# Output projection with its whole weight on chip, one token tile after another, and block-sum transfers issued in other places

## The chip, the cores and the metric

The kernel runs on one core of a Trainium2 chip. The time is the device time of one execution, in microseconds (us); less is better. The engines are PE (TensorE, matmuls and transposes), DVE (VectorE), ACT (ScalarE), POOL (GpSimd) and SP (SyncE, which issues most of the transfers here). PEclk is the clock that PE was granted, as a share of 2.4 GHz.

## What is computed

One block of a streaming encoder over 1024 tokens of width 1024, in float32. Three mixers (a gated convolution, differential attention in four heads, gated linear attention, GLA) read one normed input; then comes the output projection, a second norm, and an MLP of 4096 hidden columns:

```python
def reference(x, ln1_g, w_in, ..., w_out, ln2_g, w_mlp1, w_mlp2):
    h = rms_norm(x, ln1_g[l])
    z = h @ w_in[l]
    ...
    y = jnp.concatenate([y_conv, y_diff, y_gla], axis=-1)
    x = x + y @ w_out[l]
    h2 = rms_norm(x, ln2_g[l])
    x = x + jnp.square(jax.nn.relu(h2 @ w_mlp1[l])) @ w_mlp2[l]
    return x
```

## The kernel before, in words

**Precision and matmuls.** A float32 operand is split into a high part (`hi`, cast by ACT, line 136) and a low part (`lo`, the rest, by DVE, line 137). A product is three matmuls (`mm3`, lines 155 to 158): high by low, high by high, low by high, all added into one PSUM bank. Weights come from DRAM to a staging tile of 512 KB (`stage()`, the tag "st", two buffers), are split from there into `hi` and `lo` tiles (four buffers of each tag) and the staging buffer is free for the next load. All of these loads are issued on SP's queue in one order.

**Stages.** Norm and transposes of x into hT; projections and GLA (lines 352 to 516, with the q and k projections woven in); four attention heads (line 529), whose results go to DRAM (`ydram`); the convolution; then the part that matters here. `yT`, the mixers' result transposed and split, is loaded from ydram for six of its eight 128-row blocks and computed for two (lines 668 to 680).

**Output projection (lines 724 to 734).** The loop runs over four column blocks `nb` of 256 columns; each takes one weight (two staged pieces of w_out, 512 rows by 256 columns, line 144) and inside it goes over the eight token tiles `tt`. A step is 24 matmuls of 256 columns, the addition to the residual `x1[tt]` on DVE, the sum of squares on ACT, and for nb < 3 one `next_sum`. The tile `g2` with the norm's gain takes a buffer of the tag "st". In the last column block, `h2_tile(tt)` follows each step: statistics, scaling by DVE (`xn`), eight transposes on PE, a copy into the blocks b11, b21, b12, b22, a store of x1 to DRAM (`x1d`), and for the first four tiles differences and splits for H6 and H5. `h2_sums` makes the other operands of the MLP: H3, H7, H2, H4, H1.

**MLP.** The first product runs block-wise with seven products per block q (i = 6, 5, 3, 7, 2, 4, 1) of 24 matmuls with 512 columns; each needs one staged weight piece (`w1_operand`, line 757). The products 6 and 5 of q = 0 and 1 come first (NPRE = 2), the first of them together with the last tiles' transposes. Then the second product (`pso`).

**Block sums.** Some of the MLP's operands are sums of blocks of w_mlp1 and w_mlp2, built in DRAM by transfers that POOL issues: copies and accumulating transfers of 1 MB, 64 steps in a fixed order (`BlockSums.steps`, lines 111 to 119). `next_sum(when)` (line 128) lets POOL copy one element of a tile, so that POOL waits for that tile, and then issues the next step. Before, 8 steps are paced by the GLA output tiles (every second of 16), 32 by the attention (eight per head) and 24 by the projection.

Of the kernel before, what the change touches and what calls it, by code (L numbers as in the profile page):

```python
# [9 lines left out]
F32 = mybir.dt.float32  # L10
F32R = mybir.dt.float32r
# [25 lines left out]
def hybrid_block(ctx, tc, x, ln1_g, w_in, conv_w, q_norm_g, k_norm_g, diff_lambda, diff_subln_g,  # L37
# [316 lines left out]
    for tt in range(NT):  # L354
        ps = gemm_b(wb, hT, tt)
        nc.scalar.copy(gv[:, tt, :], ps[:, 0:256])
    wb = load_w(w_in, C_GK, 256)
# [116 lines left out]
    def gla_out(g):  # L474
# [18 lines left out]
        if g % 2 == 1:  # L493
            next_sum(ssg[0:1, tt * 4 + hh:tt * 4 + hh + 1])
# [172 lines left out]
    wo0 = load_w(w_out, 0, 256)  # L667
# [20 lines left out]
    x1 = [xp.tile([P, D], F32, name=f"x1_{tt}") for tt in range(NT)]  # L688
# [5 lines left out]

    b21, b11, b12, b22 = act_f32("b21", "ah"), act_f32("b11", "ah"), act_f32("b12", "al"), act_f32("b22", "al")
    hb = ((b11, b21), (b12, b22))
    H = {i: act_pair(actp, f"H{i}") for i in (6, 5)}
    g2 = wpool.tile([P, D], F32, name="g2", tag="st", bufs=2)
    nc.sync.dma_start(g2, ln2_g[0:1, :].broadcast_to([P, D]))
    for tt in range(NT):  # L700
        nc.sync.dma_start(x1[tt], x2[tt * P:(tt + 1) * P, :])
    ss2 = xp.tile([P, NT, 4], F32, name="ss2")

    def h2_tile(tt):
        r = norm_stats(ss2[:, tt, :], 4, xp)
# [11 lines left out]
        if th == 0:  # L717
            d6 = xp.tile([P, 4, P], F32, name="d6", tag="xn", bufs=2)
            nc.vector.tensor_tensor(d6, b11[:, :, osl], b21[:, :, osl], op=ALU.subtract)
            split(*[v[:, :, osl] for v in H[6]], d6)  # L720
            split(*[v[:, :, osl] for v in H[5]], b21[:, :, osl])
        return t_.ins

    for nb in range(4):
        wb = wo0 if nb == 0 else load_w(w_out, nb * 256, 256)
        for tt in range(NT):
            ps = gemm_b(wb, yT, tt, 256, (6, 7, 2, 3, 4, 5, 0, 1))
            xv = x1[tt][:, nb * 256:(nb + 1) * 256]
            nc.vector.tensor_tensor(xv, xv, ps[:, 0:256], op=ALU.add)
            nc.scalar.activation(ps[:, 0:256], xv, AF.Square, accum_out=ss2[:, tt, nb:nb + 1])  # L730
            if nb < 3:
                next_sum(ss2[0:1, tt, nb:nb + 1])
            if nb == 3 and tt < NT - 1:
                h2_tile(tt)


    H.update({i: act_pair(yp, f"H{i}") for i in (3, 7, 4, 2)})

    def h2_sums():
        for i in range(4):  # L740
            o = slice(i * P, (i + 1) * P)
            v11, v12, v21, v22 = (b[:, :, o] for b in (b11, b12, b21, b22))
            split(*[v[:, :, o] for v in H[3]], v12)
            split(*[v[:, :, o] for v in H[7]], v22)
            nc.vector.tensor_tensor(v11, v11, v12, op=ALU.subtract)
            nc.vector.tensor_tensor(v21, v21, v11, op=ALU.subtract)
            nc.vector.tensor_tensor(v22, v22, v21, op=ALU.subtract)
            split(*[v[:, :, o] for v in H[2]], v22)
            split(*[v[:, :, o] for v in H[4]], v21)
        H[1] = act_pair(actp, "H1")  # L750
        for i in range(4):
            o = slice(i * P, (i + 1) * P)
            split(*[v[:, :, o] for v in H[1]], b11[:, :, o])
# [27 lines left out]
    pre = []  # L781
    w = w1_operand(0, 6)
    pre.append([prod(w, e, 6, "mm", 3) for e in range(2)])
    w = w1_operand(0, 5)
    with tc.issue_after(last_mm.ins):
        h2_end = h2_tile(NT - 1)
    with tc.issue_after(h2_end):
        pre.append([prod(w, e, 5, "s", 2) for e in range(2)])
# [39 lines left out]
    for q in range(NPRE):  # L828
        p6, p5 = pre if q == 0 else (prods(q, 6), prods(q, 5))
        first[q] = [out65(2 * q + e, p6[e], p5[e]) for e in range(2)]  # L830
# [149 lines left out]
```

## Time and profile before

| | before |
|---|---|
| median of 3 runs | 1267.23 us (1264.94 to 1267.30) |
| the profiled execution: time, span | 1265.83 us, 1264.1 us |
| PE busy, share of the span | 1197.6 us, 95% |
| DVE, ACT, POOL busy | 743.8, 522.8, 65.7 us |
| mean granted clock | 0.972 |
| chain that ended last, by engine | PE 78%, DMA 10%, DVE 6%, ACT 4% |
| of it, loads of w_out | 6% |

The span runs from the first to the last instruction; the profiled execution's own time is a little longer. A chain is followed back from the last instruction, at each step to what released it. Matmul records overlap on PE, so that a busy PE is not a PE at its peak.

### The profile page before, as it was taken

How to read it: one execution, taken by the hardware profiler on the slowest of the kernel's cores; microseconds unless marked ns; L12 is line 12 of the kernel's file. 1: busy time of each engine (PE TensorE's matmuls, PEld its weight loads, DVE VectorE, ACT ScalarE, POOL GpSimd, SP SyncE). 2: the span in 40 equal slices, each digit the busy share in tenths (PEclk: the TensorE clock that was granted, in tenths of full speed). 3: DMA queues.
4: the chain of work that ended last, by engine and by line, in shares of the span. 5: the costliest groups of instructions: out<-in, count | busy, mean ns of one | idle time of the engine just before them, and what ended most of it. 6: DMA issues, size and time to landing. Idle time of an engine off the chain costs nothing.

```text
span 1264.1 us, 17602 instructions
## 1 busy us (share of the span) xinstructions
PE 1197.6 (95%) x6803; PEld 1029.7 (81%) x6803; DVE 743.8 (59%) x1366; ACT 522.8 (41%) x1019; POOL 65.7 (5%) x147
## 2 busy tenths in 40 slices
PE   6999999999999999676689999999999999999998
PEld 6897899998988788576668888888888888888887
DVE  6616654568677873111597866776666555554553
ACT  6621233557566642111475343344433333333332
POOL 1000000020102112122000000000000000000000
PEclk8999999999999999778789999999999999999999
DMA  6211244197819778999734656565599995655000
GB/s 203 84 34 34 68 163 163 46 211 237 184 50 220 211 227 262 217 267 266 194 125 162 220 184 203 192 204 173 180 315 353 387 363 200 228 210 197 32 34 33
DMA packets 118961, 231.92 MB, mean 183 GB/s; under 512 B 7357, under 2 KB 53470, under 8 KB 115550
## 3 DMA queue, kind: packets, MB, share of 16 engines
q1 hardware_dynamic: 104286, 163.69, 38.1%
q0 software_dynamic: 14592, 67.11, 22.0%
q8 instruction: 53, 0.87, 0.3%
q14 instruction: 30, 0.25, 0.1%
HBM read 189.89 MB, written 108.00 MB: 236 GB/s over the span
## 4 chain that ended last, share of the span: by engine, by line
PE 78%; DMA 10%; DVE 6%; ACT 4%; issue 1%; SPq 1%; ACTq 0%; DVEq 0%
PE pso L158 8%; PE pso L156 8%; PE pso L157 8%; PE psp L156 8%; PE psp L157 8%; PE psp L158 8%; DMA wst<-in_w_out_dram 6%; PE ps_mm L156 6%; PE ps_mm L158 6%; PE ps_mm L157 6%; PE ps_av L605 3%; DMA wst<-in_w_mlp_dram 2%; PE ps_tr L597 1%; PE ps_s L575 1%; DMA wst<-ydram 1%; PE ps_s L576 1%
## 5 line engine op out<-in xcount | busy, mean ns | idle before, releaser
L157 PE MATMUL pso<-o2h 128*128 128x512 f32 x448 | 174.3, 389 | 0.0
L156 PE MATMUL pso<-o2l,o2h 128*128 128x512 f32 x448 | 174.3, 389 | 0.0
L158 PE MATMUL pso<-o2h,o2l 128*128 128x512 f32 x448 | 174.3, 389 | 0.0
L156 PE MATMUL ps_mm<-wlo,hTh 128*128 128x256 f32 (+1 forms) x512 | 147.8, 289 | 3.8 <-ACT hTh L201 3.8
L137 DVE TENSOR_TENSOR o2l<-f,o2h 128x1024 fp32r<-128x1024 f32 x56 | 68.6, 1225 | 139.4 <-ACT o2h L136 139.4
L157 PE MATMUL ps_mm<-whi,hTh 128*128 128x256 f32 (+1 forms) x512 | 147.1, 287 | 0.0
L158 PE MATMUL ps_mm<-whi,hTl 128*128 128x256 f32 (+1 forms) x512 | 146.2, 286 | 0.0
L136 ACT CAST o2h<-f 128x1024 fp32r<-128x1024 f32 x56 | 58.8, 1051 | 190.5 <-PE pso L157 186.6
L156 PE MATMUL ps_mm<-wlo,yTh 128*128 128x256 f32 x256 | 80.2, 313 | 32.5 <-ACT ps_mm L730 26.8
L137 DVE TENSOR_TENSOR wlo<-wst,whi 128x1024 fp32r<-128x1024 f32 x34 | 41.6, 1224 | 114.5 <-ACT whi L136 112.0
L136 ACT CAST w1h<-wst 128x1024 fp32r<-128x1024 f32 x56 | 58.9, 1053 | 106.8 <-PE psp L157 86.9
L156 PEld LDWEIGHTS ps_mm<-wlo,hTh 128*128 128x128 f32 x512 | 97.0, 190 | 7.0 <-ACT hTh L201 4.7
L157 PEld LDWEIGHTS pso<-o2h 128*128 128x128 f32 x448 | 84.1, 188 | 17.6
L158 PEld LDWEIGHTS pso<-o2h,o2l 128*128 128x128 f32 x448 | 84.1, 188 | 17.5
L156 PEld LDWEIGHTS pso<-o2l,o2h 128*128 128x128 f32 x448 | 84.1, 188 | 17.3
L158 PEld LDWEIGHTS ps_mm<-whi,hTl 128*128 128x128 f32 x512 | 97.4, 190 | 0.7 <-DVE hTl L202 0.2
L157 PEld LDWEIGHTS ps_mm<-whi,hTh 128*128 128x128 f32 x512 | 97.1, 190 | 0.9 <-issue 0.3
L815 DVE TENSOR_TENSOR s<-psp,s 128x512 f32<-128x512 f32 x96 | 64.7, 689 | 51.0 <-PE psp L158 46.0
L137 DVE TENSOR_TENSOR w1l<-wst,w1h 128x1024 fp32r<-128x1024 f32 x56 | 68.4, 1221 | 35.1 <-ACT w1h L136 35.1
L156 PEld LDWEIGHTS ps_mm<-wlo,yTh 128*128 128x128 f32 x256 | 55.5, 217 | 33.8 <-ACT ps_mm L730 27.9
L158 PE MATMUL ps_mm<-whi,yTl 128*128 128x256 f32 x256 | 78.3, 306 | 0.0
L157 PE MATMUL ps_mm<-whi,yTh 128*128 128x256 f32 x256 | 78.3, 306 | 0.0
(284 smaller groups left out, 2631.5 us busy)
## 6 DMA issues: line engine op xcount, KB each, us to landing
f<-fdram SPq DMA_DIRECT2D x28, 1024.0 KB
w1s<-in_w_mlp_dram POOLq DMA_DIRECT2D x24, 1024.0 KB, 9.8
w2s<-in_w_mlp_dram POOLq DMA_DIRECT2D x24, 1024.0 KB, 17.6
wst<-w1s SPq DMA_DIRECT2D x32, 512.0 KB
w<-w2s SPq DMA_DIRECT2D x16, 1024.0 KB
wst<-in_w_in_dram SPq DMA_DIRECT2D x26, 512.0 KB
wst<-in_w_mlp_dram SPq DMA_DIRECT2D x24, 512.0 KB
fdram<-s SPq DMA_DIRECT2D x48, 256.0 KB
```

The lines of the kernel that those rows point to most:

```text
L136: nc.scalar.copy(hi, src)
L137: return nc.vector.tensor_tensor(lo, src, hi.bitcast(F32), op=ALU.subtract)
L156: nc.tensor.matmul(ps, lh, rl, start=first, stop=False)
L157: nc.tensor.matmul(ps, lh, rh, start=False, stop=False)
L158: return nc.tensor.matmul(ps, ll, rh, start=False, stop=last)
L575: nc.tensor.matmul(ps[:, 0:w], qi, kll[c][:, j * 512:j * 512 + w], start=True, stop=False)
L576: nc.tensor.matmul(ps[:, 0:w], qi, khh[c][:, j * 512:j * 512 + w], start=False, stop=True)
L597: nc.tensor.transpose(tp[:, b * P:(b + 1) * P], pc[0][:, (b0 + b) * P:(b0 + b + 1) * P], ident)
L605: nc.tensor.matmul(av[:, 0:P], aT[:, b * P:(b + 1) * P], v[:, kb, hh * P:hh * P + P], start=(kb == 0), stop=(kb == i))
L815: nc.vector.tensor_tensor(dst, a_, b_, op=op)
```

## The change

The projection now goes over the token tiles, with two halves `nh` of 512 columns each. The weight is loaded in eight pieces of 256 rows by 512 columns (`load_wo`): the four of the first half into the tiles "hi" and "lo", the four of the second half into tiles that hT has left. The first three token tiles take the first half one after another, then the second half; from tile 3 on, each tile takes both. `h2_tile` of a finished tile comes under the matmuls of the next. x1 has four buffers instead of eight and each tile is loaded when it is needed; `g2` has a tile of its own. Splits for H6 and H5 are collected after tile 3, differences are made per tile from tile 4 on, and four weights of the MLP's first products are loaded ahead. Of the block sums, the 24 of the projection are gone: 8 are paced by the gv projection, 16 instead of 8 by the GLA tiles, 32 by the attention as before, and 8 by the MLP's blocks q.

```diff
@@ -354,6 +354,7 @@
     for tt in range(NT):
         ps = gemm_b(wb, hT, tt)
         nc.scalar.copy(gv[:, tt, :], ps[:, 0:256])
+        next_sum(gv[0:1, tt, 0:1])
@@ -490,8 +491,7 @@
-        if g % 2 == 1:
-            next_sum(ssg[0:1, tt * 4 + hh:tt * 4 + hh + 1])
+        next_sum(ssg[0:1, tt * 4 + hh:tt * 4 + hh + 1])
@@ -664,7 +664,19 @@
-    wo0 = load_w(w_out, 0, 256)
+    def load_wo(j, nh, hi, lo):
+        st = stage().rearrange("p (c n) -> p c n", c=2)
+        nc.sync.dma_start(st, w_out[j * 256:(j + 1) * 256, nh * 512:nh * 512 + 512].rearrange("(c p) n -> p c n", p=P))
+        split(hi, lo, st)
+        return hi, lo
+    def load_wo0(j):
+        return load_wo(j, 0, wpool.tile([P, 2, 512], F32R, name="woh", tag="hi", bufs=4),
+                       wpool.tile([P, 2, 512], F32R, name="wol", tag="lo", bufs=4))
+    wo = [{j: load_wo0(j) for j in (3, 1)}, {}]
     yT = act_tiles(yp, "yT")
     for kc in (6, 7, 2, 3, 4, 5):
         st = stage()[:, 0:T]
@@ -685,24 +697,35 @@
-    x1 = [xp.tile([P, D], F32, name=f"x1_{tt}") for tt in range(NT)]
...
+    wo[0].update({j: load_wo0(j) for j in (2, 0)})
+    x1 = {}
+    def x1_tile(tt):
+        x1[tt] = xp.tile([P, D], F32, name="x1", tag="x1", bufs=4)
+        nc.sync.dma_start(x1[tt], x2[tt * P:(tt + 1) * P, :])
+    for tt in range(2):
+        x1_tile(tt)
+    wo1 = [act_pair(actp, "wo1") for kh in range(2)]
+    for j in (3, 1, 2, 0):
+        js = slice((j % 2) * 2, (j % 2) * 2 + 2)
+        wo[1][j] = load_wo(j, 1, wo1[j // 2][0][:, js, :], wo1[j // 2][1][:, js, :])
+    x1_tile(2)
     b21, b11, b12, b22 = act_f32("b21", "ah"), act_f32("b11", "ah"), act_f32("b12", "al"), act_f32("b22", "al")
     hb = ((b11, b21), (b12, b22))
-    H = {i: act_pair(actp, f"H{i}") for i in (6, 5)}
-    g2 = wpool.tile([P, D], F32, name="g2", tag="st", bufs=2)
+    H = {}
+    g2 = xp.tile([P, D], F32, name="g2")
     nc.sync.dma_start(g2, ln2_g[0:1, :].broadcast_to([P, D]))
-    for tt in range(NT):
-        nc.sync.dma_start(x1[tt], x2[tt * P:(tt + 1) * P, :])
-    ss2 = xp.tile([P, NT, 4], F32, name="ss2")
+    ss2 = xp.tile([P, NT, 2], F32, name="ss2")
@@ -714,43 +737,70 @@
-        if th == 0:
-            d6 = xp.tile([P, 4, P], F32, name="d6", tag="xn", bufs=2)
...
-    for nb in range(4):
-        wb = wo0 if nb == 0 else load_w(w_out, nb * 256, 256)
-        for tt in range(NT):
-            ps = gemm_b(wb, yT, tt, 256, (6, 7, 2, 3, 4, 5, 0, 1))
...
-            nc.scalar.activation(ps[:, 0:256], xv, AF.Square, accum_out=ss2[:, tt, nb:nb + 1])
-            if nb < 3:
-                next_sum(ss2[0:1, tt, nb:nb + 1])
-            if nb == 3 and tt < NT - 1:
-                h2_tile(tt)
-    H.update({i: act_pair(yp, f"H{i}") for i in (3, 7, 4, 2)})
-    def h2_sums():
+    def h2_first():
+        for i in (6, 5):
+            H[i] = act_pair(yp, f"H{i}")
         for i in range(4):
             o = slice(i * P, (i + 1) * P)
-            v11, v12, v21, v22 = (b[:, :, o] for b in (b11, b12, b21, b22))
-            split(*[v[:, :, o] for v in H[3]], v12)
-            split(*[v[:, :, o] for v in H[7]], v22)
-            nc.vector.tensor_tensor(v11, v11, v12, op=ALU.subtract)
-            nc.vector.tensor_tensor(v21, v21, v11, op=ALU.subtract)
-            nc.vector.tensor_tensor(v22, v22, v21, op=ALU.subtract)
-            split(*[v[:, :, o] for v in H[2]], v22)
-            split(*[v[:, :, o] for v in H[4]], v21)
+            d6 = xp.tile([P, 4, P], F32, name="d6", tag="xn", bufs=2)
+            nc.vector.tensor_tensor(d6, b11[:, :, o], b21[:, :, o], op=ALU.subtract)
+            split(*[v[:, :, o] for v in H[6]], d6)
+            split(*[v[:, :, o] for v in H[5]], b21[:, :, o])
+    def h2_diffs(i):
+        o = slice(i * P, (i + 1) * P)
+        nc.vector.tensor_tensor(b11[:, :, o], b11[:, :, o], b12[:, :, o], op=ALU.subtract)
+        nc.vector.tensor_tensor(b21[:, :, o], b21[:, :, o], b11[:, :, o], op=ALU.subtract)
+    def gemm_o(tt, nh):
+        ps = ps_mm()
+        th, o = tt // 4, (tt % 4) * P
+        ks = (6, 7, 2, 3, 4, 5, 0, 1)
+        for kc in ks:
+            hi, lo = wo[nh][kc // 2]
+            ah, al = yT[th][kc // 4]
+            mm3(ps, ah[:, kc % 4, o:o + P], al[:, kc % 4, o:o + P], hi[:, kc % 2, :], lo[:, kc % 2, :],
+                kc == ks[0], kc == ks[-1])
+        return ps
+    NB = 3
+    waiting = []
+    for tt, nh in [(t, h) for h in range(2) for t in range(NB)] + [(t, h) for t in range(NB, NT) for h in range(2)]:
+        if tt not in x1:
+            x1_tile(tt)
+        ps = gemm_o(tt, nh)
+        xv = x1[tt][:, nh * 512:nh * 512 + 512]
+        nc.vector.tensor_tensor(xv, xv, ps, op=ALU.add)
+        nc.scalar.activation(ps, xv, AF.Square, accum_out=ss2[:, tt, nh:nh + 1])
+        if waiting:
+            t = waiting.pop(0)
+            h2_tile(t)
+            if t == 3:
+                h2_first()
+            if t >= 4:
+                h2_diffs(t - 4)
+        if nh == 1:
+            waiting.append(tt)
+    def h2_sums():
+        h2_diffs(3)
+        for i in (3, 7):
+            H[i] = act_pair(yp, f"H{i}")
+        H[4] = act_pair(actp, "H4")
+        H[2] = act_pair(actp, "H2")
+        parts = (slice(0, 3 * P), slice(3 * P, 4 * P))
+        for o in parts:
+            split(*[v[:, :, o] for v in H[3]], b12[:, :, o])
+        for o in parts:
+            split(*[v[:, :, o] for v in H[7]], b22[:, :, o])
+        nc.vector.tensor_tensor(b22, b22, b21, op=ALU.subtract)
+        split(*H[2], b22)
+        split(*H[4], b21)
         H[1] = act_pair(actp, "H1")
-        for i in range(4):
-            o = slice(i * P, (i + 1) * P)
-            split(*[v[:, :, o] for v in H[1]], b11[:, :, o])
+        split(*H[1], b11)
@@ -778,14 +828,12 @@
-    pre = []
-    w = w1_operand(0, 6)
-    pre.append([prod(w, e, 6, "mm", 3) for e in range(2)])
-    w = w1_operand(0, 5)
+    pw = {(q, i): w1_operand(q, i) for q in range(2) for i in (6, 5)}
+    pre = {(0, 6): [prod(pw[0, 6], e, 6, "mm", 3) for e in range(2)]}
     with tc.issue_after(last_mm.ins):
         h2_end = h2_tile(NT - 1)
     with tc.issue_after(h2_end):
-        pre.append([prod(w, e, 5, "s", 2) for e in range(2)])
+        pre[0, 5] = [prod(pw[0, 5], e, 5, "s", 2) for e in range(2)]
     h2_sums()
@@ -826,7 +874,7 @@
-        p6, p5 = pre if q == 0 else (prods(q, 6), prods(q, 5))
+        p6, p5 = [pre.get((q, i)) or [prod(pw[q, i], e, i, *BANKS[i]) for e in range(2)] for i in (6, 5)]
         first[q] = [out65(2 * q + e, p6[e], p5[e]) for e in range(2)]
@@ -873,6 +921,7 @@
             f_store(2, mp, d2)
+        next_sum(f[0][2][0:1, 0:1])
```

On SP's queue, from the first pieces of w_out on. Before (line 144 loads w_out, 671 ydram, 699 the gain g, 701 and 716 x and its store, 759 the MLP's weights):

```order
L144 DMA wst<-in_w_out_dram 128x4x256 x2
L215 DMA ydram<-yt 128x512 x2
L671 DMA wst<-ydram 128x1024 x3
L215 DMA ydram<-yt 128x512 x2
L671 DMA wst<-ydram 128x1024 x3
L699 DMA g_5382<-in_ln_g_dram 128x1024
L144 DMA wst<-in_w_out_dram 128x4x256
L701 DMA x_0_5366<-in_x_dram 128x1024
```

And now (671 loads w_out, 683 ydram, 711 and 739 x and its store, 724 the gain, 809 the MLP's weights):

```order
L671 DMA wst<-in_w_out_dram 128x2x512 x2
L215 DMA ydram<-yt 128x512 x2
L683 DMA wst<-ydram 128x1024 x3
L215 DMA ydram<-yt 128x512 x2
L683 DMA wst<-ydram 128x1024 x3
L671 DMA wst<-in_w_out_dram 128x2x512 x3
L711 DMA x_5410<-in_x_dram 128x1024
L711 DMA x_5412<-in_x_dram 128x1024
L671 DMA wst<-in_w_out_dram 128x2x512 x2
L711 DMA x_5434<-in_x_dram 128x1024
L724 DMA g_5440<-in_ln_g_dram 128x1024
L671 DMA wst<-in_w_out_dram 128x2x512
```

The gain's load no longer stands between the staged pieces; three pieces follow ydram at once, and x comes tile by tile between the rest.

On POOL, from the memsets of the GLA's tiles to the first sums (L116 copies a block, L119 accumulates onto it). Before:

```order
L459 MEMSET att_1386 128x256
L310 TENSOR_TENSOR lsum<-e_base,lsum 1x2
L375 MEMSET S 128x64 x2
L130 COPY paced<-ssg 1x1
L116 DMA w1s_98<-in_w_mlp_dram 128x2048
L130 COPY paced<-ssg 1x1
```

And now:

```order
L130 COPY paced<-gv 1x1
L116 DMA w1s_99<-in_w_mlp_dram 128x2048
L376 MEMSET S 128x64 x2
L130 COPY paced<-ssg 1x1
L119 DMA w1s_98<-in_w_mlp_dram 128x2048
```

The first eight steps wait for gv's tiles, ahead of the memsets of S, and the GLA's tiles pace accumulations.

On DVE, around the last token tile (x, y_lnx and xn of the tile, b the blocks, H operands of the MLP). Before:

```order
L711 SCALAR_TENSOR_TENSOR xn<-x_6_5372,y_lnx,g_5382 128x512 x2
L137 TENSOR_TENSOR H3l<-b_5376,H3h 128x4x128
L137 TENSOR_TENSOR H7l<-b_5377,H7h 128x4x128
L83 TENSOR_TENSOR t_lnx<-y_lnx 128x1
L137 TENSOR_TENSOR H4l<-b_5374,H4h 128x4x128
L84 TENSOR_TENSOR t_lnx<-t_lnx,mln 128x1
L747 TENSOR_TENSOR b_5377<-b_5377,b_5374 128x4x128
L85 TENSOR_SCALAR t_lnx<-t_lnx 128x1
L137 TENSOR_TENSOR H3l<-b_5376,H3h 128x4x128
L86 TENSOR_TENSOR y_lnx<-y_lnx,t_lnx 128x1
L137 TENSOR_TENSOR H7l<-b_5377,H7h 128x4x128
L711 SCALAR_TENSOR_TENSOR xn<-x_7_5373,y_lnx,g_5382 128x512 x2
```

And now:

```order
L137 TENSOR_TENSOR H3l<-b_5438,H3h 128x4x384
L775 TENSOR_TENSOR x_6041<-x_6041,ps_mm 128x512
L137 TENSOR_TENSOR H7l<-b_5439,H7h 128x4x384
L186 TENSOR_REDUCE m_6179<-ss_5442 128x1
L190 TENSOR_SCALAR mln<-m_6179 128x1
L83 TENSOR_TENSOR t_lnx<-y_lnx 128x1
L84 TENSOR_TENSOR t_lnx<-t_lnx,mln 128x1
L85 TENSOR_SCALAR t_lnx<-t_lnx 128x1
L86 TENSOR_TENSOR y_lnx<-y_lnx,t_lnx 128x1
L734 SCALAR_TENSOR_TENSOR xn<-x_6041,y_lnx,g_5440 128x512 x2
L137 TENSOR_TENSOR w1l<-wst,w1h 128x1024
L754 TENSOR_TENSOR b_5437<-b_5437,b_5438 128x4x128
```

Three quarters of H3 and H7 are split ahead of the last tile's statistics, in one piece each, and H2, H4 and H1 come after it.

## Rows read from the trace of the kernel before

**Rows 1.** Busy time by stretch; columns as in the line that begins with core 0.
```profile
core 0: us, PE busy (x) PEld busy (x) DVE busy (x) ACT busy (x) POOL busy (x), PEclk, DMA share, GB/s
58.00:82.00 24.00, 23.99 (x202) 23.66 (x201) 1.65 (x4) 9.38 (x20) 0.00 (x0) 1.00 0.07 21
...
140.00:237.00 97.00, 96.70 (x816) 90.11 (x816) 41.16 (x107) 31.30 (x93) 6.74 (x17) 1.00 0.36 121
237.00:457.00 220.00, 215.63 (x1459) 187.80 (x1459) 169.33 (x489) 139.50 (x368) 28.58 (x62) 1.00 0.71 178
480.20:669.20 189.00, 141.27 (x930) 133.39 (x929) 75.46 (x162) 59.56 (x148) 25.32 (x48) 0.84 0.87 221
669.20:950.00 280.80, 280.80 (x1226) 229.93 (x1225) 193.55 (x257) 112.76 (x153) 0.00 (x0) 1.00 0.62 206
```

**Rows 2.** Timeline of PE: start, length, what.
```profile
463.96 1.06 PE L620 MATMUL ps_tr<-ident,o 128*128 128x128 f32 x8
464.78 0.48 PE L156 MATMUL ps_mm<-hTl,whi 128*128 128x512 f32 x1
...
480.21 0.27 PE L156 MATMUL ps_mm<-wlo,yTh 128*128 128x256 f32 x1
...
482.95 0.28 PE L158 MATMUL ps_mm<-whi,yTl 128*128 128x256 f32 x1
...
669.17 0.40 PE L156 MATMUL psp<-H3l,w1h 128*128 128x512 f32 x1
```

**Rows 3.** Chain of waits from 476 to 660 us: start, length, what.
```profile
481.68 3.75 DMA wst<-in_w_out_dram
485.51 1.06 ACT whi L136
...
487.85 18.66 DMA wst<-in_w_out_dram
...
522.05 1.23 DVE wlo L137
523.30 11.04 DMA wst<-in_w_out_dram
...
536.75 23.14 DMA wst<-in_w_out_dram
...
576.58 21.20 DMA wst<-in_w_mlp_dram
```

**Rows 4.** Timeline of SP's queue near 480 us.
```profile
478.22 0.33 SPq L699 DMA_DIRECT2D g<-in_ln_g_dram  x1
481.68 0.38 SPq L144 DMA_DIRECT2D wst<-in_w_out_dram  x1
482.16 4.23 SPq L701 DMA_DIRECT2D x<-in_x_dram  x8
```

**Rows 5.** View of waits, 480.2 to 669.2 us: total, times, longest.
```profile
ACT whi L136 <- DMA wst<-in_w_out_dram: 54.7, 6, 12.4
...
PE ps_tr L714 <- DVE xn L711: 15.1, 4, 6.4
```

**Rows 6.** Transfer queues (packets, MB, share of 16 engines): the span, then 480.2 to 669.2.
```profile
q0 software_dynamic: 14592, 67.11, 22.0%
...
q0 software_dynamic: 8704, 25.17, 60.9%
```

**Rows 7.** Timelines of SP's queue and ACT: w_in loads and casts.
```profile
83.39 2.07 SPq L144 DMA_DIRECT2D wst<-in_w_in_dram  x2
...
207.85 3.19 SPq L144 DMA_DIRECT2D wst<-in_w_in_dram  x2
...
103.47 1.05 ACT L136 CAST whi<-wst 128x1024 fp32r<-128x1024 f32 x1 [0.35 <-PE ps_mm L157]
...
233.07 1.05 ACT L136 CAST whi<-wst 128x1024 fp32r<-128x1024 f32 x1 [1.05 <-PE ps_mm L158]
```

**Rows 8.** View of waits, 665 to 950 us.
```profile
ACT w1h L136 <- PE psp L157: 86.5, 47, 3.3
```

More of the change, by code (lines that the diff above doesn't have):

```diff
@@ L693, in act_pair @@
         return (pool.tile([P, 4, 512], F32R, name=f"{nm}h", tag="ah"), pool.tile([P, 4, 512], F32R, name=f"{nm}l", tag="al"))
+    wo[0].update({j: load_wo0(j) for j in (2, 0)})
[10 more added lines that the diff above has]
+    x1_tile(2)
     b21, b11, b12, b22 = act_f32("b21", "ah"), act_f32("b11", "ah"), act_f32("b12", "al"), act_f32("b22", "al")
     hb = ((b11, b21), (b12, b22))
-    H = {i: act_pair(actp, f"H{i}") for i in (6, 5)}
-    g2 = wpool.tile([P, D], F32, name="g2", tag="st", bufs=2)
+    H = {}
+    g2 = xp.tile([P, D], F32, name="g2")
     nc.sync.dma_start(g2, ln2_g[0:1, :].broadcast_to([P, D]))
-    for tt in range(NT):
-        nc.sync.dma_start(x1[tt], x2[tt * P:(tt + 1) * P, :])
-    ss2 = xp.tile([P, NT, 4], F32, name="ss2")
+    ss2 = xp.tile([P, NT, 2], F32, name="ss2")
     def h2_tile(tt):
-        r = norm_stats(ss2[:, tt, :], 4, xp)
+        r = norm_stats(ss2[:, tt, :], 2, xp)
         th, o = tt // 4, (tt % 4) * P
@@ L716, in h2_tile @@
         nc.sync.dma_start(x1d[tt], x1[tt])
-        if th == 0:
-            d6 = xp.tile([P, 4, P], F32, name="d6", tag="xn", bufs=2)
-            nc.vector.tensor_tensor(d6, b11[:, :, osl], b21[:, :, osl], op=ALU.subtract)
-            split(*[v[:, :, osl] for v in H[6]], d6)
-            split(*[v[:, :, osl] for v in H[5]], b21[:, :, osl])
-        return t_.ins
-    for nb in range(4):
-        wb = wo0 if nb == 0 else load_w(w_out, nb * 256, 256)
-        for tt in range(NT):
-            ps = gemm_b(wb, yT, tt, 256, (6, 7, 2, 3, 4, 5, 0, 1))
-            xv = x1[tt][:, nb * 256:(nb + 1) * 256]
-            nc.vector.tensor_tensor(xv, xv, ps[:, 0:256], op=ALU.add)
-            nc.scalar.activation(ps[:, 0:256], xv, AF.Square, accum_out=ss2[:, tt, nb:nb + 1])
-            if nb < 3:
-                next_sum(ss2[0:1, tt, nb:nb + 1])
-            if nb == 3 and tt < NT - 1:
-                h2_tile(tt)
```

## The prediction

> **What bounds the kernel now.** I read the stretches first [rows 1]. From 58 to 457 us and from 669.2 to 950 us TensorE is busy nearly all the time at a granted clock of 1.00. The one poor stretch runs from 480.2, the first output-projection matmul, to 669.2, the first matmul of the MLP's product with H3 [rows 2]: 189.0 us, PE busy for 141.27 of them, clock 0.84 (part of it at 1.2 instead of 2.4 GHz), and the DMA engines busy 0.87 of the time. Everything that this change rewrites in the projection lies between these two matmuls, so this interval is the unit of the sum.
>
> The chain of waits inside it [rows 3] is one repeating sentence: a 512 KB piece of w_out lands after 11 to 23 us, ScalarE casts it (1.06 us), VectorE subtracts (1.23 us), and only then is the next piece issued. The very first piece landed in 3.75 us. Two things make the rest slow. On SP's queue g takes the second of the two "st" buffers at 478.22 and holds it to the end of the stage [rows 4], so six pieces of w_out go through one buffer, one after another; ScalarE waited 54.7 us for them [rows 5]. And the sums' queue holds 60.9% of the 16 engines in this interval [rows 6]; these are the 24 block sums that the projection starts, three per token tile.
>
> **The dense time of the same work.** Matmul records overlap, so a row's duration is not its price; the distance between starts is. The last 66 matmuls of 512 columns before the projection start from 464.78 to 480.21: 0.234 us each. The first 24 of 256 columns start from 480.21 to 482.95, 23 distances: 0.119 us [rows 2]. So the 768 narrow matmuls would have been 91.5 us of dense PE time, and the 384 wide ones are 384 x 0.234 = 89.8 us. **The wider matmul itself is worth 1.7 us**; the rest of the gain has to come from waits. Eight transposes took 0.82 us from first start to the next matmul's and the pipeline restarts a little late, say 0.93 us; eight token tiles of them are 7.5 us. The 96 products with H6 and H5 for q = 0 and 1 that come before H3 are 96 x 0.234 = 22.4 us. Together 119.7 us, where 189.0 are spent now: 69.3 us to be had, less what new waits take.
>
> **The waits, before and after.** Removed: the 24 sums, and g from the staging buffers (it gets its own tile), so w_out's pieces alternate between two buffers. The number of w_out pieces stays eight; two are still loaded before ydram's. The new order needs all four pieces of the first column half at once, though, where the old one needed two.
>
> At the start: buffer A is free at 478.22 and buffer B at 481.68 (the issue times of g and of the next piece [rows 4]). With 3.75 us to land and 1.06 + 1.23 us to split [rows 3], the third piece could be ready at 484.3; ScalarE and VectorE still split yT's last piece, which I let push it to 485.2. The fourth is ready at 487.8, as a piece is now. PE starts at 480.21, has 12 matmuls with the pieces that it holds (to 483.0), waits 2.2 us, does 6, and waits 1.2 us: **3.4 us of stall**. The other half's four pieces follow through the same two buffers, ready at 491.3, 493.9, 497.3 and 499.9; PE needs the first at 500.4, because three tiles of the first half come ahead. The slack is real but thin.
>
> In the middle: a tile's statistics, scaling and transposes stand under the next tile's 24 or 48 matmuls (5.6 or 11.2 us), where PE now waited 15.1 us for xn [rows 5]. I cost them at nothing; the cover is PE's own matmuls, and with VectorE late they would show as the xn waits of now. Tiles 4 to 7 of x1 reuse four buffers, so each load waits until the store of a tile four earlier has landed: at 3.75 us for each of the two, tile 4 is there some 8 us after tile 0's scaling at about 510, and is added to at about 534. Behind that wait on SP's queue stand stores and later tiles, with the same slack, and no weight for this stage.
>
> At the end: VectorE has about 14,300 columns of splits and differences between tile 7's first half and H3, at 1.23 us per 1,024 some 17 us, plus 3 us of small operations, under 120 matmuls (28 us). But the splits of three quarters of H3 and H7 stand ahead of tile 7's statistics on both engines. Casts of 1,536 columns at 1.6 us and subtractions at 1.85 us each put xn about 8.5 us behind the last projection matmul, and PE has 28 products (6.5 us) to fill with: **2 us of stall**, between 0 and 5.
>
> **Where the sums go.** A sum takes 22.0% of the span's 1264.1 us over 64, that is 4.35 us of all 16 engines [rows 6]. Eight start 2.86 us apart under the gv projection (58 to 82 us), where DMA is 0.07 busy [rows 1]: a backlog of some 35 us that ends near 95. The only loads it meets are issued at 83.39 and cast at 103.47 [rows 7]. Sixteen instead of eight start under the gated linear attention (DMA share 0.36 now [rows 1]); of the loads there the tightest is issued at 207.85 and cast at 233.07, 25 us later, against a worst landing of 23.14 us [rows 3, 7]. POOL takes one step at a time and an accumulation waits there for the copy under it; behind it on POOL stand only sums, one iota and two memsets of S. The last eight start under the MLP, one per q, into a DMA share of 0.62 [rows 1]; ScalarE waits there for PE to free a weight buffer, 86.5 us in 47 waits, and the view of waits names no load [rows 8]. For all three places together: below, nothing (a load that is early anyway gains nothing); above, 10 us, if a load in each of two places lands 5 us late. I take 2 us, near the lower end, because each load has 20 us or more.
>
> The Trainium skill (DMA: Bandwidth & Descriptors, section "Queues, rings and completion order") says that every DMA engine takes turns between the queues that have work, packet by packet. By that a load beside sums would keep half the engines and land in some 7.5 us (an estimate, twice 3.75), and the 2 us would be 0. The trace does not agree: with no x load ahead of it a piece took 11.04 us [rows 3]. By the same rule the first rival below, where every piece lands beside sums, would end at 1210 instead of its 1221.
>
> **Sum.** 119.7 + 3.4 + 2 + 2 = 127.1 us in place of 189.0: 61.9 us less. The profiled execution took 1265.83 us (span 1264.1), so 1203.9; the median of the runs shown is 1.4 us above that execution. I predict **1204 us**. No stall at all and the 0.229 us per matmul that the MLP shows (280.8 us for 1226 [rows 1]) would give 1194.
>
> **Rivals.** *The weights stay late.* The sums under the last attention head may still run at 480 (accumulations now, copies before), and x and x1d share the engines. If pieces land in 11.04 us, the two buffers deliver every 13.3 us: PE waits until 495.0 for the fourth piece and until 521.7 for the eighth, 20.4 us of stall instead of 3.4, and the time is 1221. For it: every piece but the first in this stage was that slow. Against it: no new sum starts here, and the 3.75 us piece landed while the attention's last copies had hardly drained. Chance 0.14.
>
> *The sums bite under the MLP; slower than before.* Its loads follow each other every 5.6 us through two buffers. If a sum in flight makes two of them take 23.14 us, the worst landing [rows 3], each of the eight sums costs 23.1 - 11.2 = 11.9 us where no split weights are in hand: 95 us, 1204 + 95 = 1299. It decides from 7.8 us per sum on, where the 62 us are used up. Against it: four buffers of split weights, so three products of 5.6 us in hand, loads that nothing waits for now [rows 8], and only one sum in some 35 us. Chance 0.04.
>
> *Wide matmuls overlap further.* If 512 columns issued at the distance of 256, 384 x 0.115 = 44 us would go too: 1160. Both distances are read at clock 1.00 with no wait between [rows 2], so 0.02. The Trainium skill (TensorE: Matmul & The Clock Gate, "Back-to-back issue gap") gives about 131 ns for sustained 512-column matmuls, by which the pass would be 50 us (an estimate); the 234 ns here do not bear it out.
>
> *Early sums bite under the linear attention*, 5 to 10 us at the loads of [rows 7]: 1209 to 1214, chance 0.04. *The change does nothing*, because the stage is held by something that no row shows: 0.01.
>
> **Numbers.** My forecast, 1196 to 1210, has 0.75. The range 1196 to 1222 adds the late weights and the bite under the linear attention, and leaves out a tenth or so at both ends together. A difference of 0.2% (2.5 us) is about what can be told from none. Faster: 0.75 + 0.14 + 0.02 + 0.04 = 0.95; same 0.01; slower 0.04.
>
> **What would show it.** Right: the interval from the first projection matmul to the first H3 product near 125 us at a clock of 1.00; w_out pieces landing in about 4 us, two at a time; two short PE waits near its start on the third and fourth piece; a wait of about 2 us on xn before tile 7's transposes; TensorE still at 1.00 and full in 669.2 to 950's counterpart. Wrong: w_out pieces at 10 us or more with PE waiting for them (the first rival), ScalarE waiting for w1 loads in the MLP (the second), or a PE hole at 100 or 235 us (the fourth).

## The result and the profile after

The changed kernel takes **1209.58 us** (median of 4 runs, 1206.35 to 1210.74) against 1267.26 us of the kernel before (4 runs, 1264.94 to 1267.61): ratio 0.9544, 95% interval 0.9523 to 0.9566. That is 57.7 us less; the forecast was 1204, the range 1196 to 1222. The profiled execution took 1209.38 us, its span is 1207.7 us and its mean granted clock 0.991 (before 1265.83, 1264.1 and 0.972).

The page of the changed kernel: TensorE's busy time, its granted clock in 40 slices, and the sums' queue.

```profile
PE 1180.9 (98%) x6419; PEld 997.7 (83%) x6419; DVE 744.7 (62%) x1334; ACT 516.8 (43%) x974; POOL 65.7 (5%) x147
...
PEclk8999999999999999999999999999999999999999
...
q0 software_dynamic: 14592, 67.11, 23.7%
```

The same 67.11 MB of sums are moved [rows 6], and no slice but the first shows a granted clock under 0.9 any more (a 9 stands for 0.9 and above).

The view of stretches of the changed kernel; the columns are those of [rows 1]. The first line spans the linear attention's last steps, the next the new projection interval (first projection matmul to first product with H3), the third the rest of the MLP up to the second matrix.

```profile
205.00:250.00 45.00, 39.78 (x324) 38.21 (x323) 14.89 (x30) 16.75 (x37) 3.00 (x6) 0.96 0.70 162
490.00:612.10 122.10, 118.50 (x546) 96.26 (x544) 75.07 (x131) 54.66 (x103) 0.70 (x2) 1.00 0.42 146
612.10:899.00 286.90, 286.90 (x1249) 234.43 (x1248) 200.27 (x264) 115.69 (x158) 6.83 (x14) 1.00 0.73 228
```

The interval's two ends, from the timeline of PE (start, length, what):

```profile
489.95 0.40 PE L156 MATMUL ps_mm<-wol,yTh 128*128 128x512 f32 x1
...
612.10 0.39 PE L156 MATMUL psp<-H3l,w1h 128*128 128x512 f32 x1
```

It lasted 189.0 us [rows 1, 2] and lasts 122.1 now: 66.9 us less, with the clock up from 0.84 to 1.00 and the DMA share down from 0.87 to 0.42. The view of waits for 480 to 520 us has one line for PE, the sum, the number and the longest of its waits:

```profile
PE ps_mm L156 <- DVE wol L137: 3.2, 2, 2.1
```

The piece that ends the first of them, in the chain of waits (start, length, what):

```profile
488.56 3.97 DMA wst<-in_w_out_dram
...
492.61 1.05 ACT woh L136
493.69 1.22 DVE wol L137
```

A piece lands in 3.97 us where all but the first took 11.04 to 23.14 [rows 3]. PE waits twice, 2.1 us for the third piece and 1.1 us for the fourth.

But the interval begins 9.8 us later than before (490.0 against 480.2), and most of that, 6.4 us, opens between 216 us (the end of the linear attention's steps) and 249.7 us, the first attention matmul (240.0 before). The view of waits for 205 to 252 us:

```profile
ACT yt L514 <- DMA ydram<-yt: 12.5, 1, 12.5
...
PE ps_mm L156 <- ACT dv L437: 4.6, 1, 4.6
```

The chain of the same stretch (start, length, what):

```profile
215.98 0.70 ACT yt L514
216.69 15.45 DMA ydram<-yt
...
232.22 0.56 ACT yt L514
...
233.51 0.27 ACT dv L437
```

The output of the linear attention is stored through two yt buffers. The third yt tile needs the first one's buffer, whose store of 256 KB takes 15.45 us beside the sums. That is not the price of 256 KB alone: two w_in loads of 512 KB stand ahead of the store on SP's queue (timeline of SP: start, length, what):

```profile
211.16 3.18 SPq L144 DMA_DIRECT2D wst<-in_w_in_dram  x2
216.69 17.17 SPq L215 DMA_DIRECT2D ydram<-yt  x4
```

And the whole queue crawls. The view of transfer queues for 211 to 227 us (packets, MB, share of 16 engines; q0 carries the sums, q1 what SP issues):

```profile
q0 software_dynamic: 391, 2.91, 92.3%
q1 hardware_dynamic: 403, 0.41, 8.7%
```

In these 16 us not even one of the two loads' 512 KB went through. ScalarE stands for 12.5 us, the dv copies behind it on its queue come late, PE has no PSUM bank to write for 4.6 us, and after its pause runs below full clock (0.72 from 233 to 239 us). The whole ledger, in span: -66.9 (interval) + 9.8 (before it) + 0.7 (MLP; before, 286.2 from 669.2 to 955.4) = -56.4 = 1207.7 - 1264.1; the second MLP matrix takes 308.7 us in both.

### The profile page after: what moved, and what is told of

It reads as the page before. It is cut to its first block, busy times and chain, and to the rows that moved or that the text cites. A ratio compares the mean times of both kernels' runs of the same rounds, so it can differ in the third digit from the quotient of the medians.

```text
span 1207.7 us, 16752 instructions
## 1 busy us (share of the span) xinstructions
PE 1180.9 (98%) x6419; PEld 997.7 (83%) x6419; DVE 744.7 (62%) x1334; ACT 516.8 (43%) x974; POOL 65.7 (5%) x147
## 3 DMA queue, kind: packets, MB, share of 16 engines
q0 software_dynamic: 14592, 67.11, 23.7%
## 4 chain that ended last, share of the span: by engine, by line
PE 88%; DVE 5%; DMA 3%; ACT 3%; issue 1%; SPq 1%; ACTq 0%
PE psp L156 9%; PE psp L157 9%; PE ps_mm L156 9%; PE psp L158 9%; PE pso L158 8%; PE pso L157 8%; PE pso L156 8%; PE ps_mm L158 8%; PE ps_mm L157 8%; PE ps_av L605 3%; PE ps_tr L597 1%; PE ps_s L575 1%; DMA ydram<-yt 1%; PE ps_s L576 1%; PE ps_s L471 1%; DMA wst<-ydram 1%
## 5 line engine op out<-in xcount | busy, mean ns | idle before, releaser
L156 PEld LDWEIGHTS pso<-o2l,o2h 128*128 128x128 f32 x448 | 84.1, 188 | 17.5
L137 DVE TENSOR_TENSOR wlo<-wst,whi 128x1024 fp32r<-128x1024 f32 x26 | 31.8, 1224 | 60.5 <-ACT whi L136 58.0
L137 DVE TENSOR_TENSOR o2l<-w,o2h 128x1024 fp32r<-128x1024 f32 x56 | 68.2, 1219 | 0.0
L157 PE MATMUL ps_mm<-hTh,whi 128*128 128x512 f32 x160 | 64.3, 402 | 0.0
L158 PE MATMUL ps_mm<-hTh,wlo 128*128 128x512 f32 x160 | 64.0, 400 | 0.0
L156 PE MATMUL ps_mm<-hTl,whi 128*128 128x512 f32 x160 | 64.0, 400 | 0.0
## 6 DMA issues: line engine op xcount, KB each, us to landing
w2s<-in_w_mlp_dram POOLq DMA_DIRECT2D x24, 1024.0 KB, 11.1
```

Of the source, the lines that this page charges most:

```text
L137: return nc.vector.tensor_tensor(lo, src, hi.bitcast(F32), op=ALU.subtract)
L156: nc.tensor.matmul(ps, lh, rl, start=first, stop=False)
L157: nc.tensor.matmul(ps, lh, rh, start=False, stop=False)
L158: return nc.tensor.matmul(ps, ll, rh, start=False, stop=last)
```

## The experiments

Theory: the gain is the w_out pieces landing alone, with two buffers; the loss is the y store beside the sums of the linear attention. Every edit below is on the changed kernel unless it says otherwise. Ratios are to the kernel before; the change has 0.9544 [0.9523, 0.9566].

### e1: a buffer for each y store

```
-            yt = y_tile()
+            yt = gp.tile([P, 512], F32, name="yt", tag="yt", bufs=2) if th == 0 else y_tile()
             nc.scalar.activation(yt, tp, AF.Copy, scale=gn_col)
```

(sqg, a scratch tile, has one buffer instead of two to make room.)

> Edit: the first two yt tiles of the linear attention's output get buffers of their own, so that the third one no longer waits for the first y store to land. Theory (the 12.5 us that ScalarE stands at 216 us of the changed kernel, for a 256 KB store that takes 15.45 us beside two sums, is the place of most of the 6.4 us lost between 216 and 250 us): that wait goes, the dv copies follow at once, the first attention matmul comes at 242 to 245 us instead of 249.7, and the time is 1202 to 1205 us. Rival (the sums under the linear attention hold up all transfers there, and the store is only the first one that something waits for): the wait goes, the next transfer's wait takes its place, the first attention matmul stays at 247 to 250 us, and the time is 1207 to 1210 us.

Measured: 1203.41 us, ratio 0.9499 [0.9486, 0.9512]. The y store is gone from the waits, nothing took its place, and the first attention matmul starts at 242.7. The theory holds: this wait is worth 6.2 us. The sums still run there (DMA share 0.88 from 140 to 237 us in both kernels); what cost was the one place where an engine waits for a transfer issued a moment before. SP's queue still has only 11.4% of the engines from 211 to 227 us, with the w_in loads on it, and nothing waits for those. Whether the store, issued ahead of these loads, would land in time beside the sums was not run.

### e2: the last four sums of the linear attention under the MLP

```
-        next_sum(ssg[0:1, tt * 4 + hh:tt * 4 + hh + 1])
+        if g < 12:
+            next_sum(ssg[0:1, tt * 4 + hh:tt * 4 + hh + 1])
...
         next_sum(f[0][2][0:1, 0:1])
+        if q < 4:
+            next_sum(f[1][2][0:1, 0:1])
```

> Edit: the last four of the linear attention's 16 sums are left out there and begun under the first four q of the MLP, two a q. Theory (the store is slow because the last sums still run at 216 us): the stores take 3 to 6 us, ScalarE's wait falls from 12.5 us to under 3, the time is 1202 to 1205 us, and the MLP's 253 us between 640 and 893 stay dense. Rival one (the sums cost by their number and not by their place): 1208 to 1210 us. Rival two (the MLP has no room for four more sums of 4.35 us): it loses some 10 us and the time is 1215 us or more.

Measured: **1200.77 us**, ratio 0.9479 [0.9461, 0.9497], 1.2 us better than the theory's range. The view of stretches of this kernel:

```profile
140.00:237.00 97.00, 96.70 (x815) 89.97 (x814) 41.61 (x112) 29.92 (x92) 11.73 (x25) 1.00 0.65 166
```

PE is back at 96.70 of 97 us at full clock, as before [rows 1]; the changed kernel had 92.09 of 97 at 0.97. ScalarE's wait for the store is gone and the first attention matmul starts at 242.1. From 211 to 227 us SP's queue moves 2.09 MB here, against 0.41 MB in the changed kernel. The first projection matmul to the first H3 product takes 120.9 us, as PE's waits for w_out fall from 3.2 to 1.5. The MLP up to its second matrix takes 287.3 us instead of 286.9 with four sums more. So the number of sums does not set the price here; what stands beside a sum does.

### e3: only the sums moved (edit on the kernel before)

```
         nc.scalar.copy(gv[:, tt, :], ps[:, 0:256])
+        next_sum(gv[0:1, tt, 0:1])
...
-        if g % 2 == 1:
-            next_sum(ssg[0:1, tt * 4 + hh:tt * 4 + hh + 1])
+        next_sum(ssg[0:1, tt * 4 + hh:tt * 4 + hh + 1])
...
-            if nb < 3:
-                next_sum(ss2[0:1, tt, nb:nb + 1])
...
             f_store(2, mp, d2)
+        next_sum(f[0][2][0:1, 0:1])
```

> Edit: the kernel before with its sums begun where the change begins them, and its projection loop left alone (column block by column block, weights one block ahead, the norm after the last block). Theory (the 24 sums in the projection make the w_out transfers slow; without them two pieces of 4 us and their casts, 12.4 us, fit under the 22.8 us of a column block, and only the norm of the last block, some 3 to 20 us that VectorE takes longer than TensorE, and 1.7 us for the narrow matmuls remain): the waits for w_out fall from 54.7 us to under 5, the interval from the first projection matmul to the first H3 product is 127 to 145 us, and the time is 1214 to 1233 us. Rival (loading one block ahead through one stage buffer is what holds the projection up, whatever else runs): the waits for w_out stay above 25 us and the time is 1240 us or more.

Measured: 1221.62 us, ratio 0.9638 [0.9621, 0.9655]. The view of waits of this kernel's interval (487.6 to 619.8 us, 132.2 us):

```profile
PE ps_tr L714 <- DVE xn L711: 6.3, 5, 3.9
...
ACT whi L136 <- DMA wst<-in_w_out_dram: 4.3, 3, 2.8
```

ScalarE's 54.7 us for w_out [rows 5] are 4.3, through one staging buffer and with the old loop. Moving the sums alone gives 46 of the 58 us, although it also brings the y store's wait (12.8 us here). The rival, that the single buffer held the stage up, falls. One loss stays open: the second MLP matrix takes 314.1 us instead of 308.7, with one wait (view of waits, 900 to 1220 us):

```profile
PE pso L156 <- DVE o2l L137: 3.5, 1, 3.5
```

ScalarE stands there 8.3 us for a load of f. The changed kernel has the same eight sums under the MLP and no such wait.

### e4: only the loop rewritten

```
-        next_sum(gv[0:1, tt, 0:1])
...
+        if g % 2 == 1:
+            next_sum(ssg[0:1, tt * 4 + hh:tt * 4 + hh + 1])
...
         nc.scalar.activation(ps, xv, AF.Square, accum_out=ss2[:, tt, nh:nh + 1])
+        for _ in range(nh + 1):
+            next_sum(ss2[0:1, tt, nh:nh + 1])
...
-        next_sum(f[0][2][0:1, 0:1])
```

> Edit: the changed kernel with its 24 sums back in the projection (one behind each first half of a token tile, two behind each second), 8 in the linear attention and none in the gv products or the MLP. Theory (sums beside the w_out pieces make each take 11 to 23 us instead of 4, and the second half of the weight, four pieces through two stage buffers, is wanted 17 us after the start): TensorE waits 10 to 30 us for w_out, and the time is 1213 to 1235 us. Rival (the whole weight on chip and the tile order are enough, the early pieces are there before the sums begin): no wait over 5 us, and 1202 to 1206 us, better than the change since the linear attention gets its 8 sums back.

Measured: 1232.8 us, ratio 0.9731 [0.9705, 0.9756]; interval 152.3 us (480.1 to 632.4). The time is the theory's, the place is not: TensorE waits 6.5 us for w_out, not 10 to 30. The view of waits on PE, 480 to 634 us:

```profile
PE psp L156 <- ACT ps_mm L776: 11.1, 1, 11.1
PE ps_mm L156 <- DVE wo1l L137: 4.4, 1, 4.4
...
PE ps_mm L156 <- DVE wol L137: 2.1, 2, 1.1
```

And on ScalarE:

```profile
ACT w1h L136 <- DMA wst<-in_w_mlp_dram: 18.5, 2, 10.3
ACT wo1h L136 <- DMA wst<-in_w_out_dram: 13.0, 4, 9.4
ACT s L869 <- DMA x1d<-x: 6.3, 1, 6.3
```

Two pieces of the chain at the interval's end:

```profile
600.93 22.37 DMA x1d<-x
...
623.40 0.04 ACT s L869
```

ScalarE stands 13.0 us for w_out. Most is lost at the end: from the first H6 product to the first H3 product 47.4 us (23.1 in the changed kernel), which is 24 of the interval's 30 us. MLP weights and a store of x1d taking 22.37 us stand there beside the last sums, and PE waits 11.1 us for a PSUM bank that ScalarE, behind its weight casts, frees late. The loop alone gives 35 us, the sums alone 46, both 58: the two overlap. That both take PE off the same slow pieces is the likely reason, and no run separates it. With the sums gone from the projection, the loop is worth 12 us on top: in the profiled spans 10.1 us in the interval (132.2 against 122.1) and the 5.4 us at e3's second matrix, less 2.3 us ahead of the interval and 0.6 in the MLP.

### e5: one staging buffer again

```
+    g2 = wpool.tile([P, D], F32, name="g2", tag="st", bufs=2)
+    nc.sync.dma_start(g2, ln2_g[0:1, :].broadcast_to([P, D]))
     wo[0].update({j: load_wo0(j) for j in (2, 0)})
...
-    g2 = xp.tile([P, D], F32, name="g2")
-    nc.sync.dma_start(g2, ln2_g[0:1, :].broadcast_to([P, D]))
```

> Edit: the changed kernel with the gain vector of the second norm back in one of the two stage buffers, loaded ahead of the third weight piece, so that six of the eight w_out pieces pass through one buffer. Theory (a piece takes 4 us to land and 2.3 us of casts, and with one buffer these follow one another, 6.2 us a piece; the fourth piece then comes about 3 us later, and the last two of the second half some 9 us after TensorE wants them): TensorE waits 8 to 16 us more between 490 and 530 us, and the time is 1217 to 1227 us. Rival (without sums beside them the pieces are early enough through one buffer, and the second buffer is worth nothing): 1208 to 1212 us.

Measured: 1218.25 us, ratio 0.9622 [0.9598, 0.9646]: 8.7 us for the second buffer. PE's waits on PE's view in the interval:

```profile
PE ps_mm L156 <- DVE wol L137: 3.9, 1, 3.9
PE ps_mm L156 <- DVE wo1l L137: 3.4, 2, 2.1
```

That is 7.3 us of waits instead of 3.2; of the 4.4 us that remain of the interval's 8.5 (130.6 against 122.1), up to 3.4 are granted clock, from three stretches of 6 us:

```profile
494.00:500.00 6.00, 3.40 (x9) 2.75 (x10) 1.23 (x1) 1.04 (x1) 0.00 (x0) 0.72 0.65 230
...
512.00:518.00 6.00, 3.90 (x15) 2.81 (x14) 1.22 (x1) 1.04 (x1) 0.00 (x0) 0.88 0.20 67
518.00:524.00 6.00, 6.00 (x23) 4.72 (x22) 1.23 (x1) 1.05 (x1) 0.00 (x0) 0.84 0.27 95
```

(0.28 + 0.12 + 0.16 of 6 us each; a part of the first is the wait itself.) The theory's time holds at its lower end, but not its sum: it had 8 to 16 us of further waits and no clock, where 4.1 us of waits came.

### e6: the wide products cut in two

```
+        for c in range(2):
+            cs = slice(c * 256, c * 256 + 256)
...
+                mm3(ps[:, cs], ah[:, kc % 4, o:o + P], al[:, kc % 4, o:o + P], hi[:, kc % 2, cs], lo[:, kc % 2, cs],
...
```

> Edit: each 512-column product of the changed projection as two of 256 columns, one after the other. Theory (768 products of 119 ns against 384 of 234 ns: the width is worth 1.7 us): 1210 to 1213 us. Rival (half as many weight loads are the gain of the loop, since a load before each narrow product holds TensorE up): 1225 us or more.

Measured: 1213.26 us, ratio 0.9582 [0.9559, 0.9606]: 3.7 us slower than the change, 0.3 us above the theory's range, and the intervals overlap by 0.0007. The profiled execution is the slowest of the four (1216.99 us); its interval is 129.1 us, 7.0 more, of which PE's first wait (3.7 us in one piece instead of 3.2 in two) is 0.5, the clock around it (0.82 and 0.61 in two stretches of 6 us) up to 3.4, and waits for xn at the end 1.7; some 1.4 us or a little more are left for the width itself. The theory's 1.7 us fit, as an estimate and not as a measured difference; the rival of 15 us or more falls.

### e7 and e8: more sums under the MLP

```
+        if g % 2 == 1:
+            next_sum(ssg[0:1, tt * 4 + hh:tt * 4 + hh + 1])
...
+        next_sum(f[1][2][0:1, 0:1])
```

e8 takes the eight sums of gv away as well and begins three a q.

> Edit: the changed kernel with the linear attention's sums back to one for every second step (8), and two a q under the MLP (16 there). Theory (after twelve sums in the linear attention nothing waited for its stores, so eight there are worth no more than the 2 us by which its steps still came later than before, and 16 in the MLP leave its TensorE dense): the first attention matmul at 240 to 242 us and 1197 to 1201 us. Rival (16 sums in the MLP bite): the 287 us from the first H3 product to the first product of the second MLP matrix grow by 5 us or more, and the time is 1205 us or more.

> Edit: as before this one, but no sums under the gv products either, and three a q under the MLP (24 there). The MLP's transfers without sums fill 0.58 of its DMA time (0.72 with one sum of 4.35 us in each 31.6 us of a q), three sums add 13.1 us a q, which makes 0.99. Theory (a stage whose transfers fill the DMA engines to 0.99 makes TensorE wait for its weights): the MLP's 287 us grow by 5 to 20 us and the time is 1203 to 1220 us. Rival (transfers from several queues overlap so well that a share of one is not yet a limit): the MLP stays within 2 us and the time is 1195 to 1200 us.

Measured: e7 1209.84 us, ratio 0.9556 [0.9534, 0.9578]; e8 1230.34 us, ratio 0.9702 [0.9674, 0.9729].

e7 misses its range, and its rival's place is wrong too: the MLP takes 286.9 us, as with 8 sums. Against e2's span (1199.1) the 8.9 us of 1208.0 are 0.8 up to the first attention matmul (242.9), 1.5 in the attention, 4.2 in the interval (125.1 against 120.9), -0.4 in the MLP and 2.8 at the start of the second matrix, where PE waits once:

```profile
PE pso L156 <- DVE o2l L137: 2.5, 1, 2.5
```

ScalarE stands there for loads of f (17.0 us in two waits). That the two sums of the last q hold these loads up is a reading, which e11 tests. In the interval PE had one wait of 3.4 us, and the granted clock fell behind it; why the third piece came later than in e2 is not shown (view of stretches, e7):

```profile
490.00:496.00 6.00, 5.16 (x12) 4.10 (x13) 3.36 (x5) 2.61 (x3) 0.00 (x0) 0.50 0.68 242
```

e8 shows the bite that the prediction's second rival described. The MLP grows from 286.9 to 303.8 us, as its theory had it, and the second matrix from 308.7 to 321.1, which it did not have; so the time lies 10 us above its range. ScalarE's first line of waits from 600 to 925 us, where the changed kernel has 7.3 us in three:

```profile
ACT w1h L136 <- DMA wst<-in_w_mlp_dram: 48.8, 12, 9.3
```

### e9 to e11: the projection's start by halves

```
+    half = [gemm_o(t, 0, None, slice(0, 4)) for t in range(2)]
...
-        ps = gemm_o(tt, nh)
+        ps = gemm_o(tt, 0, half[tt], slice(4, 8)) if nh == 0 and tt < 2 else gemm_o(tt, nh)
```

gemm_o takes a PSUM tile and the part of its weight order to do. e10 adds the edit of e2; e11 has 10 sums in the linear attention and 14 in the MLP, one in each of the last two q.

> Edit: the changed kernel with the first two token tiles of the projection taken half by half: first the products of both with the two weight pieces that are there (2 x 12 products of 234 ns, 5.6 us), then those with the third and fourth. Theory (TensorE stands 2.1 and 1.1 us for the third and fourth piece, which come 5 and 8.4 us after its first product; with 5.6 us of work ahead of the third piece both waits go): TensorE waits under 1 us there, the interval from the first projection matmul to the first H3 product is 118 to 120 us instead of 122.1, and the time is 1205 to 1208 us. Rival (the pieces are held up by the engines that cast them, and the tail of the projection is set by VectorE's norm, so that what is gained at the start is lost at the end): 1209 to 1211 us.

> Edit: the last edit and that of e2 together (12 sums in the linear attention, 12 in the MLP). Theory (the losses are in different places and add up: 8.8 us from e2, and 1.5 us, which is what TensorE still waited for w_out there): 1197.5 to 1200.5 us. Rival (the start of the projection is worth nothing there): 1200.5 to 1202 us.

> Edit: as e10, with 10 sums in the linear attention and 14 in the MLP, two a q but one in each of the last two. Theory (the 2.8 us that TensorE lost at the start of the second MLP matrix with two sums in the last q came from sums that were still running beside its first loads; with one in each of the last two q there is no such wait; and two sums fewer in the linear attention are worth nothing, since nothing waits there at 12): 1197 to 1201 us, within 1 us of e10. Rival (every sum under the MLP beyond 12 costs in the second MLP matrix or at the granted clock, wherever it stands): 1203 us or more.

Measured: e9 1207.73 us, 0.9520 [0.9498, 0.9541]; e10 **1199.82 us**, 0.9464 [0.9448, 0.9481]; e11 1200.07 us, 0.9466 [0.9446, 0.9486].

e9 is inconclusive: 1.9 us faster than the change with overlapping intervals. The time lies in the theory's range, but its trace misses the theory: PE's waits fall only to 1.8 us, the clock falls to 0.87 and 0.85 in the two stretches of 6 us from 494 on, and the interval is 122.0 us, not 118 to 120. In e10 the same edit works as meant, with no wait over 0.2 us there and an interval of 119.0 us:

```profile
PE ps_mm L156 <- DVE wol L137: 0.2, 1, 0.2
```

but the medians of e2 and e10 differ by less than their intervals tell apart. e11 stands within 1 us of e10, as its theory had it, and its trace names no wait of PE at the second matrix. That fits e7's reading, and e10, e2 and the change, with one sum in each last q, have no such wait either; but e3 has one with a single sum a q, so a sum too many in the last q is not shown to be the only cause. Each of e2, e10 and e11 beats the change by 8.8 to 9.8 us, with intervals that lie apart from its own.

## Why the prediction was right, and where it was off

**The interval (terms 119.7 + 3.4 + 2).** 125.1 us were predicted, 122.1 measured.
- *The stall at the start, 3.4 us as 2.2 and 1.2.* Measured 3.2 us as 2.1 and 1.1, from buffer times and a 3.75 us landing that came out at 3.97. The second half of the weight caused no wait of PE.
- *The stall at the end, 2 us.* The transposes of the last tile waited 0.2 us for xn; the term was 1.8 us too high.
- *The dense work, 119.7 us.* 122.1 - 3.2 - 0.2 leaves 118.7, 1.0 us less. Both the width's 1.7 us and the conclusion that the rest must come from waits stand: e6 leaves some 1.4 us or a little more for the width, e3 puts 46 us on the sums.
- *The middle at nothing.* No wait for xn over 0.2 us, and none for x1: right.
- *g's buffer.* The prediction named two causes for the slow pieces, the single buffer and the sums. e3 and e5 price them apart: the sums are the larger one, and one buffer alone is hidden in the old loop; the new loop, which wants four pieces at once, pays 8.7 us without the second.

**The place of the moved sums, 2 us.** This is the step that failed in size: the stretches outside the interval lost 10.5 us in the profiled execution (9.8 ahead of it, 0.7 in the MLP), a little more than the upper bound of 10. The prediction read the loads of w_in in the linear attention and gave the tightest 25 us of room; the tight transfer there was a store. "A load in each of two places lands 5 us late" has its counterpart in one store, 15.45 us long, with room for none of it: two yt buffers, four tiles in a row, and the dv copies behind them on ScalarE (e1: 6.2 us; e2: 8.8 us with the four sums gone from there). The kernel before told of it: its fourth yt tile already waits for a y store, so that the room was used up with half the sums (timeline of ACT, before):

```profile
220.17 0.69 ACT L514 ACTIVATE yt<-ps_tr,cols 128x512 f32<-128x512 f32 x1 [0.98 <-DMA ydram<-yt]
```

Of the rest, 1.5 us stood at the first gv copy (62.3 against 60.8 us), ahead of any sum, and 1.8 us came between there and the last step of the linear attention. Both are granted clock, with PE busy throughout (view of stretches, the changed kernel):

```profile
56.00:62.00 6.00, 6.00 (x35) 5.48 (x34) 2.95 (x4) 3.33 (x7) 0.00 (x0) 0.72 0.55 165
144.00:150.00 6.00, 6.00 (x42) 5.31 (x43) 1.06 (x3) 1.32 (x6) 1.02 (x2) 0.72 0.41 59
```

Each is 0.28 of 6 us, 1.7 us. The kernel before has 1.00 in both, and so has e5, which is the changed kernel up to there: its first gv copy is at 60.9 and its last step at 212.8 us, as before (60.8 and 212.7). So these 3.3 us are no price of the 24 sums there that every execution pays; the price of the moved sums is the other 7.1 us.

**The rivals.** *Weights late*: no, 3.97 us a piece; e4 shows slow pieces when the sums stay in the projection, though at 6.5 us of PE's waits. *Sums bite under the MLP*: no at one sum a q and none at two (286.9 us in e7), yes at three (e8), with ScalarE waiting for w1 as described, but at (303.8 - 286.9) / 24 = 0.7 us a sum, or 1.2 with the second matrix, far from the rival's 11.9. Its ground that the view names no load [rows 8] was misread. The same view, which ends just ahead of the second matrix, has a load of f for it; there e3, e7 and e8 wait:

```profile
ACT o2h L136 <- DMA f<-fdram: 3.9, 1, 3.9
```

*Wide matmuls overlap further*: no, the dense 118.7 us leave no room for it. *Early sums bite under the linear attention, 1209 to 1214, chance 0.04*: this is what happened in place, at the y store rather than at the loads that it named; its chance was too small. That the time fits it too (1209.4 in the profiled execution) is in part luck, through the 3.3 us of clock. The interval took 3.0 us less than its terms and the places 8.5 us more than theirs: the two errors partly cancel, and the 5.5 us that are left kept the time inside the forecast of 1196 to 1210.

**The Trainium skill's turn-taking rule** (DMA: Bandwidth & Descriptors, "Queues, rings and completion order") says that each DMA engine goes round the queues that have work, packet by packet. From 211 to 227 us the trace agrees: 403 packets of SP's queue against 391 of the sums. What failed is the half of the engines that the prediction made of it (an estimate); the trace that it found against the rule speaks against that estimate only. By the view's bytes a packet held 1.0 KB on SP's queue and 7.4 KB on the other, so that as many packets left SP's queue 8.7% of the engines' time. Beside the w_out piece of 11.04 us [rows 3] (before, 523.3 to 534.3 us) the view has 528 packets of 1.0 KB against 966 of 2.0 KB and a share of 17.5%: not one for one, and again far from a half.

## What to carry to other kernels

When background transfers are moved, list every transfer on which an engine waits soon after its issue in the new place, stores included, with what stands ahead of it on its queue: a store's landing time is the reuse time of its buffer, and two buffers for a burst of four tiles left no room here. Price a moved transfer by what is issued beside it, not by the share of DMA time that is free: at the same number of sums, e2 gained 8.8 us by taking four of them away from one store. And a stream that was the background of a tight stage is best held back for the last steps ahead of such a burst (e2), and perhaps ahead of the next stage's first loads (e7's last q, which is not shown apart).

## What the runs showed of the hardware that was not expected

A wait of TensorE at the projection's start cost more than its own length in several runs, through the granted clock behind it. After one wait of 3.4 us (e7) it was 0.50 over six us, that is 1.2 GHz throughout; after 3.7 (e6) 0.61, after 3.9 (e5) 0.72, parts of the stretch at 1.2 and the rest at 2.4 GHz. With waits of 2.1 and 1.1 us with work between them (the change) it stayed at 1.00 (view of stretches, the changed kernel):

```profile
490.00:496.00 6.00, 3.91 (x17) 2.88 (x16) 3.64 (x5) 2.54 (x4) 0.00 (x0) 1.00 0.51 173
496.00:502.00 6.00, 4.87 (x22) 3.71 (x21) 3.56 (x4) 2.17 (x3) 0.00 (x0) 1.00 0.90 339
```

And yet after a single 1.8 us (e9 and e11) it fell to between 0.81 and 0.90. In the changed kernel it stood at 0.72 from 56 to 62 and from 144 to 150 us with no wait at all. So the length of a wait alone does not tell here whether the clock falls. Six us at 0.50 are some 3 us of lost work, nearly as much as the wait itself; the prediction's rival of late weights counted its stalls without it.
